# Issuing the gate stores and the rotation's half swaps from ScalarE's queue instead of SyncE's

## The chip, the core and the metric

The kernel runs on one core of one Trainium2 chip. The metric is the device time of one execution in microseconds (us), the median of several runs. The core has a matrix engine (TensorE: PE, with PEld for its weight loads), VectorE (DVE), ScalarE (ACT), GpSimd (POOL) and SyncE (SP). Each engine works through its own list of instructions in order. SP computes nothing; in this kernel it issues nearly all DMAs.

## What is computed

Two encoder layers run over 768 tokens (512 of one request, 256 of another), model width 1024, all in float32. Each layer has three attention branches on the same normalised input:

```python
z = h @ w_in
cq, ckv, kr, gate_a, qkv_b, gate_b, qkv_c, gate_c, merge = jnp.split(z, cuts, axis=-1)
o_a = mla_attention(cq, ckv, kr, g_q, w_uq, g_kv, w_ukv)                       # rotated queries and keys
o_b = dilated_attention(rope(qkv_b[:, :, 0], pos), rope(qkv_b[:, :, 1], pos), qkv_b[:, :, 2])
o_c = neighbourhood_attention(qkv_c[:, :, 0], qkv_c[:, :, 1], qkv_c[:, :, 2], rpb)
mg = jax.nn.sigmoid(merge.reshape(b, s, N_BRANCH, D_MODEL))
mixed = mg[:, :, 0] * p_a + mg[:, :, 1] * p_b + mg[:, :, 2] * p_c               # p_x = (o_x * silu(gate_x)) @ w_px
return x + gate[:, None, :] * rmsnorm(mixed @ w_out, g_post)

def rope(x, pos):       # rotation: each half of a head meets the other half
    x1, x2 = x[..., :half], x[..., half:]
    return jnp.concatenate([x1 * cos - x2 * sin, x2 * cos + x1 * sin], axis=-1)
```

## The kernel before

Features lie on the 128 partitions, tokens along the free axis. A float32 product is made of three matmuls of rounded parts (high by high, high by low, low by high). For that, every weight tile that is loaded (`load_split`, L165) is cast by ACT to its high part (L177), and DVE or POOL subtract to get the low part (L160). `feat_mm` (L201) multiplies such a weight tile with the layer's input; a tile of 1024 weights per partition takes 48 matmuls.

The layers run one after the other, and in each the branches A (`branch_a`), B (`branch_b`) and C (`branch_c`), then `merge` and `project`. The program is written in that order, but a scheduler fixes each engine's list when the kernel is built: it interleaves instructions of neighbouring stages, so where an instruction stands in its engine's list is not where the source has it. Buffers come from pools with fixed numbers of slots.

Two pieces matter here.

**The rotation, `rope_tile` (L448 to L460).** ACT copies a product out of PSUM to `x` (L209, 512 columns and then 256). For the rotation a second tile `xs` is needed, in which the two halves of each head have changed places. Halves lie on different partitions, so `xs` is made by DMAs inside SBUF (L455, L456): four of 32 partitions for a tile of branch B, eight of 16 partitions for a tile of branch A. Then DVE multiplies `x` by the cosines (L458), `xs` by the sines (L459) and adds (L460). Behind that, `q_stack` and `k_stack` split the rotated tile: ACT casts (L409, L421, L422) alternate with DVE subtractions (L410, L423), and PE forms scores (L820). Branch B has 12 such tiles a layer (4 heads by 3 dilations), branch A two; both layers together 24 and 4. In the trace the tiles of branch B are `xb`, those of branch A `qr`.

**The gates ahead, `early` (L1021).** The 24 merge gates of a layer are independent of the attention. Some are computed early, to give PE work while branches wait: `merge_gate` multiplies (tiles `mg`), ACT applies Tanh (L1019) into the tile `the`, which has one buffer, and a DMA stores it to DRAM (L1027). `merge` loads them again. 35 gates go this way.

In the course of branch B, `value_pair` of branch C begins (PE tiles `vp`, L753). Its input is a token permutation of the layer's input, which ACT writes as it casts (`hc`, L923). Exponentials of branch B are L864 on ACT, the casts of its probabilities L879, L884 and L898.

DMAs issued on ACT before: 32 loads of the bias of branch C (L972, L973). All else is issued on SP.

Of the kernel before, what the change touches and what calls it, by code (L numbers as in the profile page):

```python
# [66 lines left out]
def trunk_kernel(ctx, tc, x_t, c_row, c_col, w_ada0, w_ada, cols, w_a, w_feat, w_val, w_val2, w_uqk, w_qr, w_uv, w_pj, w_o,  # L67
                 bias_s, bias_p, rope_t, rope_k, mask_b, mask_c, y_t):
    nc = tc.nc
# [18 lines left out]
    def U(tag, dt=F32, name=None):  # L88
        return pool.tile([P, T], dt, tag=tag, name=name or tag, bufs=BUFS[tag])
# [51 lines left out]
    th_scr = dram.tile([depth, 24, P, T], F32, name="th_scr")  # L141
# [65 lines left out]
    def evac(outs, dst, fn):  # L207
        for g, (o, n) in enumerate(GROUPS):
            fn(dst[:, o:o + n], outs[g])  # L209
# [238 lines left out]
    def rope_tile(outs, cos, sin, half, dst):  # L448

        x = dst  # L450
        xs = U("rp", name="xs")
        if outs:
            evac(outs, x, nc.scalar.copy)
        for b in range(0, P, 2 * half):
            nc.sync.dma_start(out=xs[b:b + half], in_=x[b + half:b + 2 * half])  # L455
            nc.sync.dma_start(out=xs[b + half:b + 2 * half], in_=x[b:b + half])  # L456
        for o, n in GROUPS:
            nc.vector.tensor_mul(x[:, o:o + n], x[:, o:o + n], cos[:, :n])  # L458
            nc.vector.tensor_mul(xs[:, o:o + n], xs[:, o:o + n], sin[:, :n])  # L459
        nc.vector.tensor_add(x, x, xs)  # L460
# [18 lines left out]
    def latents(l, h, hl):  # L479
# [87 lines left out]
        while pend:  # L567
            flip(*pend.pop(0))
        early(l, h, min(LATE_E, FILL[l][0]))
        do_jobs(gates, GATES[l][-1], c_)  # L570
        ada_gain(l)
        pend = [(j, (3, 4, 5)) for j in range(6)]
        early(l, h, FILL[l][0] - LATE_E, lambda k, mm: flips(mm))
        while pend:
            flip(*pend.pop(0))
        return cn, krs

    def branch_a(l, h_, h):
# [13 lines left out]
        va = None  # L592
        for pr in range(4):
            early(l, h, FILL[l][1 + 2 * pr])
            if pr % 2 == 0:

                (wh, wl), = load_split(w_uv[l, pr // 2], 512)[1]
                va = [U("cv", F32R, name="va") for _ in range(4)]
                for t in range(6):
                    vp = ps_mm.tile([P, 256], F32, tag="g1", name="vp")  # L600
                    n = 0
                    for k in range(2):
                        for (a, w) in ((0, wh), (0, wl), (1, wh)):
                            nc.tensor.matmul(vp, cn[3 + k][a][:, t * 128:(t + 1) * 128], w[:, k * 256:(k + 1) * 256],
                                             start=(n == 0), stop=(n == 5))
                            n += 1
                    store_v(va, t, vp)

                outs = feat_mm(w_qr[l, pr // 2], 3, cqn, name="qr")
                qr = U("rp", name="qr")  # L610
                rope_tile(outs, cos_a, sin_a, 16, qr)
                qr_hl = (U("rp", F32R, name="qrh"), U("rp", F32R, name="qrl"))
                nc.scalar.activation(qr_hl[0], qr, AF.Copy, scale=scale)
                nc.vector.scalar_tensor_tensor(qr_hl[1], qr, scale, f(qr_hl[0]), ALU.mult, ALU.subtract)
# [173 lines left out]
    def branch_b(l, h, hl):  # L788
# [4 lines left out]
        for hd in range(4):  # L793
# [10 lines left out]
            for gi, dd in enumerate((1, 4, 16)):  # L804
                outs = feat_mm(w_feat[l, F_B + hd * 3 + gi], KT, hl, name="qkb")
                x = U("rp", name="xb")
                rope_tile(outs, cos_b, sin_b, 32, x)
                xg = lambda g: x[:, GROUPS[g][0]:GROUPS[g][0] + GROUPS[g][1]]
                qs = q_stack(xg, 0, perm_b(dd))
                kb = low(0)  # L810
                ka = k_stack(xg, 1, perm_b(dd), kb, 0)
                prods = ((ka, qs), (kb, qs))
                for g, (o, n) in enumerate(GROUPS):
                    for t2 in range(0, n // P, 2):
                        sp = SP()
                        ts, dst = (pairs[g][t2 // 2] if gi == 0 else ((t2, t2 + 1), None))
                        for k, t in enumerate(ts):
                            q0 = o + (t2 * P if gi else NW[t] if g == 0 else 0)
                            for i, (w, a) in enumerate(prods):
                                nc.tensor.matmul(sp[:, k * 256:k * 256 + 256],  # L820
                                                 w[:, o + t * P:o + t * P + P], a[:, q0:q0 + 256],
                                                 start=(i == 0), stop=(i == 1))
                        if gi == 0 and g == 0:
                            mk = mb0[:, 0:3:2] if t2 == 0 else mb0[:, 1:2].to_broadcast([P, 2, 256])
                            nc.vector.tensor_add(two(dst), two(sp), mk)
                        elif gi == 0:
                            for k in range(2):
                                nc.vector.tensor_add(wins[k], sp[:, k * 256:k * 256 + 256], mb0[:, 2 * k])
                        else:
                            nc.vector.tensor_add(blocks(tbs[g][gi - 1])[:, t2:t2 + 2], blocks(sp)[:, 0:4:3],  # L830
                                                 mbd(gi, g).unsqueeze(1).to_broadcast([P, 2, P]))
# [184 lines left out]
    def merge_gate(l, idx, h, th, between=None):  # L1016
        mg = feat_mm(w_feat[l, F_MG + idx], KT, h, name="mg", between=between)
        for g, (o_, n) in enumerate(GROUPS):
            nc.scalar.activation(th[:, o_:o_ + n], mg[g], AF.Tanh, scale=0.5)  # L1019

    def early(l, h, n, between=None):  # L1021

        for _ in range(n):
            idx = 23 - len(ahead)
            th = U("f", name="the")
            merge_gate(l, idx, h, th, between)
            nc.sync.dma_start(out=th_scr[l, idx], in_=th)  # L1027
            ahead.add(idx)

    def do_jobs(jobs, n, cact):  # L1030
# [167 lines left out]
    xs = []  # L1198
    sums = Z4_()[:, :12].rearrange("p (t c) -> p t c", c=2)
    x2s = [U("cv", name="x2") for _ in range(2)]  # L1200
    for t_ in range(T // P):
        x, x2 = U("cv", name="x"), x2s[t_ // 3][:, t_ % 3 * 256:t_ % 3 * 256 + 256]
        nc.sync.dma_start(out=x, in_=x_t[t_, :, :T])
        if t_ % 3 == 0:
            nc.sync.dma_start(out=x2s[t_ // 3].rearrange("p (t c) -> p t c", c=256),
                              in_=x_t[t_:t_ + 3, :, T:].rearrange("t p c -> p t c"))
# [205 lines left out]
```

## Time and profile before

| | |
|---|---|
| median of 3 runs | 1964.03 us (1962.99 to 1964.36) |
| the profiled execution | 1966.35 us |
| its span, first to last instruction | 1964.6 us |
| PE busy | 1845.0 us, 94% of the span |
| DVE busy | 1530.9 us, 78% |
| ACT busy | 1018.6 us, 52% |
| POOL busy | 664.2 us, 34% |

Busy time is that of the engine's computing instructions. The time in which an engine's queue issues a DMA or waits is not counted as busy, so ACT's 52% leaves out what its queue spends on issuing. The profiled execution is 2.3 us above the median and its time 1.75 us above its span; sums in the prediction are made on the profiled execution and then set against the median.

### The profile page before, as it was taken

What the parts mean: (1) busy time and instruction counts of PE and PEld (TensorE: products, weight loads), DVE (VectorE), ACT (ScalarE), POOL (GpSimd) and SP (SyncE); (2) the same over time, 40 slices, a digit from 0 to 9 for tenths busy, and PEclk for the clock granted to TensorE, in tenths of its full rate; (3) what the DMA queues carried; (4) which work ended last, traced back from release to release, by engine and by line L of the source; (5) the groups of instructions that cost most, each with busy time, mean ns of one, the idle gap of its engine ahead of it and who ended that gap; (6) DMA issues with size and microseconds to landing.
All of it is one profiled execution on the core that took longest, in us unless ns stands there. A gap on an engine that the chain in (4) does not pass through costs nothing. (4 is left out here: it accounts for less than half of the span.)

```text
span 1964.6 us, 30204 instructions
## 1 busy us (share of the span) xinstructions
PE 1845.0 (94%) x10674; PEld 1638.1 (83%) x10674; DVE 1530.9 (78%) x3018; ACT 1018.6 (52%) x2123; POOL 664.2 (34%) x432
## 2 busy tenths in 40 slices
PE   7897999999989987999999999999999999987998
PEld 6886888888877876888999888889888778876898
DVE  8957768579987999896587467687699868997763
ACT  5356556356577455322464356574566684653241
POOL 6404415202221454316534024253022212454570
PEclk9998999999999999999999999999999999998999
DMA  8432241232313233445452332422222222233652
GB/s 294 150 117 62 86 139 57 71 99 82 92 54 92 79 117 115 167 143 191 140 197 89 124 99 88 135 76 86 87 85 85 88 75 89 87 107 99 217 174 71
DMA packets 94904, 221.25 MB, mean 113 GB/s; under 512 B 18096, under 2 KB 32504, under 8 KB 94752
## 3 DMA queue, kind: packets, MB, share of 16 engines
q1 hardware_dynamic: 90144, 213.02, 33.4%
q10 hardware_dynamic: 4608, 6.29, 1.1%
q8 instruction: 84, 1.38, 0.3%
q14 instruction: 68, 0.56, 0.1%
HBM read 173.78 MB, written 28.18 MB: 103 GB/s over the span
## 5 line engine op out<-in xcount | busy, mean ns | idle before, releaser
L665 POOL PARTITION_ALL_REDUCE fixed<-fixed x128 | 314.2, 2486 | 496.3 <-DVE fixed L662 337.0
L201 PE MATMUL mg<-fixed 128*128 128x512 f32 (+1 forms) x2304 | 436.2, 342 | 1.4 <-DVE o_t L397 0.7
L201 PEld LDWEIGHTS mg<-fixed 128*128 128x128 f32 x2304 | 360.3, 191 | 51.6 <-PE sp L984 1.0
L177 ACT CAST fixed<-fixed 128x512 fp32r<-128x512 f32 (+1 forms) x332 | 199.5, 606 | 339.3 <-PE mg L201 117.8
L160 DVE TENSOR_TENSOR fixed<-fixed,fixed 128x512 fp32r<-128x512 f32 (+3 forms) x309 | 224.2, 729 | 113.9 <-ACT fixed L177 110.7
L201 PE MATMUL qkb<-fixed 128*128 128x512 f32 (+1 forms) x1152 | 211.9, 338 | 0.0
L201 PEld LDWEIGHTS qkb<-fixed 128*128 128x128 f32 x1152 | 177.0, 189 | 24.2
L201 PE MATMUL gate<-fixed 128*128 128x512 f32 (+1 forms) x960 | 184.0, 341 | 1.6 <-DVE tq L830 1.3
L201 PEld LDWEIGHTS gate<-fixed 128*128 128x128 f32 x960 | 150.0, 191 | 22.0 <-DVE tq L830 1.5
L1064 PE MATMUL pp<-hi,fixed 128*128 128x512 f32 (+1 forms) x640 | 161.5, 340 | 5.0 <-ACT th L1019 4.7
L680 DVE TENSOR_TENSOR fixed<-tq,fixed 128x512 fp32r<-128x512 f32 (+1 forms) x160 | 127.9, 821 | 2.7 <-ACT fixed L679 2.5
L1064 PEld LDWEIGHTS pp<-hi,fixed 128*128 128x128 f32 x640 | 111.9, 192 | 19.9 <-ACT th L1019 5.1
L671 ACT ACTIVATE tq<-tq 128x512 f32<-128x512 f32 (+1 forms) x160 | 83.4, 545 | 82.7 <-DVE tq L670 82.5
L429 POOL MEMSET kb<- 64x768 f32 x56 | 41.1, 736 | 209.5 <-PE sp L820 121.0
L670 DVE TENSOR_TENSOR tq<-tq,fixed 128x512 f32<-128x512 f32 (+1 forms) x160 | 97.8, 660 | 16.3 <-POOL fixed L665 16.2
L1163 PE MATMUL op<-wo,fixed 128*128 128x384 f32 (+1 forms) x648 | 108.2, 320 | 1.8 <-POOL wo L160 1.8
L1064 PE MATMUL pp<-lo,fixed 128*128 128x512 f32 (+1 forms) x320 | 108.9, 341 | 0.8 <-DVE lo L160 0.8
L1163 PEld LDWEIGHTS op<-wo,fixed 128*128 128x128 f32 x648 | 101.3, 188 | 3.2 <-POOL wo L160 3.1
L311 DVE SCALAR_TENSOR_TENSOR fixed<-tm,fixed 128x768 f32<-128x768 f32 (+1 forms) x128 | 93.3, 729 | 2.1 <-DMA tm<-in_w_ada_dram 0.4
L868 POOL PARTITION_ALL_REDUCE fixed<-fixed x16 | 49.0, 3084 | 128.4 <-DVE fixed L845 65.7
L662 DVE TENSOR_TENSOR fixed<-tq 128x256 f32<-128x256 f32 (+1 forms) x128 | 79.1, 623 | 14.3 <-ACT tq L647 10.8
L679 ACT CAST fixed<-tq 128x512 fp32r<-128x512 f32 (+1 forms) x160 | 80.8, 530 | 11.0 <-PE o_ps L683 8.2
(245 smaller groups left out, 3910.7 us busy)
## 6 DMA issues: line engine op xcount, KB each, us to landing
fixed<-in_w_feat_dram SPq DMA_DIRECT2D x108, 512.0 KB
th_scr<-the SPq DMA_DIRECT2D x35, 384.0 KB
th<-th_scr SPq DMA_DIRECT2D x35, 384.0 KB
tm<-in_w_ada_dram SPq DMA_DIRECT2D x32, 384.0 KB
fixed<-in_w_val_dram SPq DMA_DIRECT2D x20, 512.0 KB
xs<-xb SPq DMA_DIRECT2D x96, 96.0 KB
fixed<-in_w_pj_dram SPq DMA_DIRECT2D x32, 256.0 KB
fixed<-in_w_o_dram SPq DMA_DIRECT2D x16, 512.0 KB
```

The costliest lines, as they stand in the source:

```text
L160: eng.tensor_sub(out, a, b)
L177: nc.scalar.copy(hi[:, :m], raw[:, o:o + m])
L201: state["mm"] = nc.tensor.matmul(outs[g], w[:, wsl], a[g], start=(i == 0 and wi == 0), stop=(i == nk - 1 and wi == 2))
L311: nc.vector.scalar_tensor_tensor(junk, x, 1.0, c, ALU.mult, ALU.mult, accum_out=ada2[:, l, i, g, j:j + 1])
L662: nc.vector.tensor_tensor(out, xs[0], xs[1], op=op)
L665: nc.gpsimd.partition_all_reduce(red, out, P, RED.max if op == ALU.max else RED.add)
L670: nc.vector.tensor_sub(x, x, m)
L671: nc.scalar.activation(x, x, AF.Exp)
L679: nc.scalar.copy(hi, x)
L680: nc.vector.tensor_sub(lo, x, f(hi))
L1064: nc.tensor.matmul(pp, w[:, ws], o[k][a][:, o_:o_ + n], start=(i == 0), stop=(i == 3 * nk - 1))
L1163: mm = nc.tensor.matmul(op[cc], m[a][g][:, k, c0:c0 + P], parts[k][cc][b], start=(k == 0 and i == 0), stop=(k == KT - 1 and i == 2))
```

## The change

Three lines change the queue that issues a DMA. What is moved, from where to where, and how much, stays the same.

```diff
@@ rope_tile
         if outs:
             evac(outs, x, nc.scalar.copy)
         for b in range(0, P, 2 * half):
-            nc.sync.dma_start(out=xs[b:b + half], in_=x[b + half:b + 2 * half])
-            nc.sync.dma_start(out=xs[b + half:b + 2 * half], in_=x[b:b + half])
+            nc.scalar.dma_start(out=xs[b:b + half], in_=x[b + half:b + 2 * half])
+            nc.scalar.dma_start(out=xs[b + half:b + 2 * half], in_=x[b:b + half])
@@ early
             merge_gate(l, idx, h, th, between)
-            nc.sync.dma_start(out=th_scr[l, idx], in_=th)
+            nc.scalar.dma_start(out=th_scr[l, idx], in_=th)
             ahead.add(idx)
```

The scheduler then makes new lists for all engines. Three places on ACT show it. First, the rotation of the first tile of branch A in layer 0 (`xs_1312` from `qr_1311`). In the kernel before, ACT's list has there:

```order
L177 CAST fixed5_72<-fixed15_73 128x512 [waits PE_49,Activation_49]
L209 COPY qr_1311<-qr1_1292 128x256 [waits PE_49]
L409 ACTIVATE qs_1357<-qn1_1338 64x256 [waits PE_49]
L177 CAST fixed5_72<-fixed15_73 128x512 [waits DMAHW0_49,PE_49,Activation_49]
L177 CAST fixed5_72<-fixed15_73 128x512 [waits PE_49,Activation_49]
```

In the changed kernel ACT's list has at the same place:

```order
L209 COPY qr_1311<-qr1_1292 128x256 [waits PE_49]
L455 DMA xs_1312<-qr_1311 16x768 [waits DMAHW6_49,Activation_49]
L409 ACTIVATE qs_1357<-qn1_1338 64x256 [waits PE_49]
L456 DMA xs_1312<-qr_1311 16x768 [waits DMAHW0_49]
L455 DMA xs_1312<-qr_1311 16x768 [waits DMAHW2_49]
L456 DMA xs_1312<-qr_1311 16x768 [waits DMAHW3_49]
L455 DMA xs_1312<-qr_1311 16x768 [waits DMAHW4_49]
L456 DMA xs_1312<-qr_1311 16x768 [waits DMAHW5_49]
L455 DMA xs_1312<-qr_1311 16x768 [waits DMAHW6_49]
L456 DMA xs_1312<-qr_1311 16x768 [waits DMAHW7_49]
L177 CAST fixed5_72<-fixed15_73 128x512 [waits PE_49] x2
```

The eight swaps now stand between the copy and the next weight casts (L177) of ACT.

Second, the eleventh tile of branch B in layer 0 (`xs_5219` from `xb_5218`). In the kernel before, ACT goes from the copy of `xb_5218` to exponentials, and then to the casts of the tile before it (`xb_5117`):

```order
L209 COPY xb_5218<-qkb0_5168 128x512 [waits PE_49]
L209 COPY xb_5218<-qkb1_5169 128x256 [waits PE_49]
L864 ACTIVATE tq_4598<-tq_4598 128x256 [waits DVE_49]
L864 ACTIVATE tq_4599<-tq_4599 128x256 [waits DVE_49]
L864 ACTIVATE tq_4596<-tq_4596 128x256 [waits DVE_49]
L864 ACTIVATE tq_4597<-tq_4597 128x256 [waits DVE_49]
L884 CAST fixed5_72<-tq_4598 128x256 [waits DVE_49,PE_49,Activation_49]
L177 CAST fixed5_72<-fixed15_73 128x512 [waits DMAHW0_49,PE_49]
L409 ACTIVATE qs_5130<-xb_5117 64x512 [waits DVE_49]
```

In the changed kernel ACT has behind the two copies of `xb_5218`:

```order
L455 DMA xs_5219<-xb_5218 32x768 [waits DVE_49,Activation_49]
L409 ACTIVATE qs_5130<-xb_5117 64x512 [waits DVE_49]
L409 ACTIVATE qs_5130<-xb_5117 64x256
L421 CAST ka_5137<-xb_5117 64x512
L422 CAST ka_5137<-xb_5117 64x512
L421 CAST ka_5137<-xb_5117 64x256
L422 CAST ka_5137<-xb_5117 64x256
L456 DMA xs_5219<-xb_5218 32x768 [waits DMAHW1_49]
L864 ACTIVATE tq_4598<-tq_4598 128x256 [waits DVE_49]
L864 ACTIVATE tq_4596<-tq_4596 128x256 [waits DVE_49]
L864 ACTIVATE tq_4599<-tq_4599 128x256 [waits DVE_49]
L455 DMA xs_5219<-xb_5218 32x768 [waits DMAHW2_49]
```

The four swaps of one tile are now spread between computing instructions that wait for DVE; the fourth stands another exponential and a weight cast further down.

Third, the twelfth tile of branch B in layer 0 (`xb_5318`) and the start of branch C's permuting casts (`hc_5549`). In the kernel before, ACT has:

```order
L209 COPY xb_5318<-qkb1_5269 128x256 [waits PE_49]
L898 CAST fixed5_72<-tq_4598 128x2x128 [waits DVE_49,PE_49]
L923 CAST hc_5549<-fixed5_72 128x512
L923 CAST hc_5549<-fixed5_72 128x256
L177 CAST fixed5_72<-fixed15_73 128x512 [waits DMAHW5_49,PE_49]
L409 ACTIVATE qs_5231<-xb_5218 64x512 [waits DMAHW6_49,DVE_49]
```

In the changed kernel ACT has at this place:

```order
L455 DMA xs_5319<-xb_5318 32x768 [waits Activation_49]
L456 DMA xs_5319<-xb_5318 32x768
L455 DMA xs_5319<-xb_5318 32x768 [waits DMAHW6_49]
L456 DMA xs_5319<-xb_5318 32x768 [waits DMAHW7_49]
L177 CAST fixed5_72<-fixed15_73 128x512 [waits PE_49]
L409 ACTIVATE qs_5231<-xb_5218 64x512 [waits DVE_49]
L409 ACTIVATE qs_5231<-xb_5218 64x256
L421 CAST ka_5238<-xb_5218 64x512 [waits Pool_49]
L422 CAST ka_5238<-xb_5218 64x512
L421 CAST ka_5238<-xb_5218 64x256
L422 CAST ka_5238<-xb_5218 64x256
L923 CAST hc_5549<-fixed5_72 128x512 [waits DMAHW3_49,DMAHW2_49,DMAHW1_49]
```

The four swaps and the six casts of `xb_5218` now stand ahead of the first cast of `hc`.

## Rows read from the trace of the kernel before

**Rows 1.** The page's busy times: us, share of the span, instructions.
```profile
PE 1845.0 (94%) x10674; PEld 1638.1 (83%) x10674; DVE 1530.9 (78%) x3018; ACT 1018.6 (52%) x2123; POOL 664.2 (34%) x432
```

**Rows 2.** What PE waited for: us in total, times, longest.
```profile
PE sp L820 <- DVE kb L423: 5.9, 5, 2.1
PE vp L753 <- ACT hc L923: 5.7, 4, 2.8
...
PE sp L820 <- ACT ka L422: 4.8, 7, 1.3
```

**Rows 3.** Stretches of layer 0: length, busy PE, PEld, DVE, ACT, POOL; clock; DMA share, GB/s.
```profile
387.00:450.00 63.00, 63.00 (x380) 55.85 (x379) 47.36 (x85) 36.00 (x68) 4.33 (x4) 1.00 0.30 90
450.00:540.00 90.00, 85.11 (x518) 74.82 (x517) 84.51 (x144) 51.76 (x90) 22.56 (x14) 1.00 0.28 87
540.00:570.00 30.00, 25.68 (x139) 21.39 (x138) 29.48 (x53) 21.67 (x40) 8.25 (x3) 0.89 0.27 73
570.00:615.00 45.00, 39.33 (x188) 31.70 (x188) 33.56 (x63) 39.40 (x64) 10.03 (x6) 1.00 0.19 60
```

**Rows 4.** Issues by tile and line: duration in ns (min/median/max), first and last start.
```profile
L455 SPq DMA_DIRECT2D xs<-xb x48: 507/542/593, 394.5 to 1562.0; - x48
L456 SPq DMA_DIRECT2D xs<-xb x48: 581/590/1672, 395.1 to 1562.7; - x48
L456 SPq DMA_DIRECT2D xs<-qr x16: 578/589/900, 130.5 to 1262.4; - x16
L1027 SPq DMA_DIRECT2D th_scr<-the x35: 319/327/530, 111.0 to 1728.3; - x35
L972 ACTq DMA_DIRECT2D bm<-in_bias_s_dram x16: 334/334/384, 599.5 to 1682.2; - x16
```

**Rows 5.** Waits of ACT and DVE for DMAs: us in total, times, longest.
```profile
ACT fixed L177 <- DMA fixed<-in_w_feat_dram: 2.0, 2, 1.4
DVE xb L458 <- DMA xs<-xb: 6.9, 4, 1.9
```

**Rows 6.** ACT in order of time where the second and third place lie.
```profile
541.51 0.84 ACT L209 COPY xb<-qkb 128x512 f32<-128x512 f32 x2
542.25 1.34 ACT L864 ACTIVATE tq<-tq 128x256 f32<-128x256 f32 x4
...
546.66 0.94 ACT L409 ACTIVATE qs<-xb 64x512 fp32r<-64x512 f32 x2 [1.75 <-DVE xb L460]
...
549.33 0.41 ACT L422 CAST ka<-xb 64x256 fp32r<-64x256 f32 x1
...
551.66 1.70 ACT L923 CAST hc<-fixed 128x512 fp32r<-128x512 f32 x2
```

**Rows 7.** SP's queue, the swaps of the eleventh tile.
```profile
542.37 0.51 SPq L455 DMA_DIRECT2D xs<-xb  x1
...
544.20 0.59 SPq L456 DMA_DIRECT2D xs<-xb  x1
```

**Rows 8.** DVE, the eleventh tile: first product and sum of the rotation.
```profile
549.00 0.70 DVE L458 TENSOR_TENSOR xb<-xb,fixed 128x512 f32<-128x512 f32 x1
...
555.18 0.95 DVE L460 TENSOR_TENSOR xb<-xb,xs 128x768 f32<-128x768 f32 x1
```

**Rows 9.** PE where branch C's value products begin.
```profile
561.96 0.49 PE L753 MATMUL vp<-fixed,hc 128*128 128x512 f32 x1 [2.76 <-ACT hc L923]
```

**Rows 10.** ACT and its queue around a bias load that it issues.
```profile
599.40 0.63 ACT L923 CAST hc<-fixed 128x256 fp32r<-128x256 f32 x1
599.52 0.38 ACTq L972 DMA_DIRECT2D bm<-in_bias_s_dram  x1
599.94 0.41 ACT L864 ACTIVATE tq<-tq 128x256 f32<-128x256 f32 x1
```

**Rows 11.** ACT, the casts behind the first rotation of branch A.
```profile
131.76 1.14 ACT L177 CAST fixed<-fixed 128x512 fp32r<-128x512 f32 x2 [1.51 <-PE kn L201]
```

**Rows 12.** PE, the gate whose weights those casts make.
```profile
138.82 8.51 PE L201 MATMUL mg<-fixed 128*128 128x512 f32 x48
```

## Prediction

> **What bounds the kernel now.** I read the page's busy times first. PE computes for 94% of the span, DVE for 78%, ACT for 52% [rows 1]: the kernel is bound by PE, and time is gained or lost where PE stands still. So the second view is the list of PE's waits. None of its large entries ends on a DMA; the ones that touch the changed code are waits for the casts and subtractions behind the rotation, 5.9 + 4.8 us, and for the permuted input of branch C, 5.7 us [rows 2].
>
> The third view is busy time by stretch, for layer 0's branch B, where 12 of a layer's 14 rotated tiles are. The reader is to see three situations [rows 3]. From 387 to 450 us PE is busy for all 63 us: whatever others do there is hidden. From 450 to 540 us PE has 4.9 us idle of 90, DVE is busy for 84.5, ACT for 51.8. From 540 to 615 us branch B runs into branch C: PE is idle for 4.3 of 30 and then 5.7 of 45 us, and ACT is busy for 39.4 of those 45. There ACT is what is waited for; the last 2 of the layer's 12 tiles fall there. In the stretch from 540 to 570 us the granted clock is 0.89 of full speed: part of it runs at the lower of the two levels (1.2 instead of 2.4 GHz), after PE had stood idle. That costs 30 x 0.11 = 3.3 us.
>
> **What the change moves, and its cost.** The issues go from SP to ACT. On SP a swap of branch B takes 0.542 and 0.590 us in turn, so four take 2.26 us; eight swaps of branch A, at 0.589, take 4.7 us; a store of a gate takes 0.327 us [rows 4]. The trace of before has no swap on ACT. It has bias loads there, 0.334 us each [rows 4], the same as what SP needs for a transfer over 128 partitions, so I take SP's durations for ACT. In total ACT's queue gets 24 x 2.26 = 54.3 us, 4 x 4.7 = 18.8 us and 35 x 0.327 = 11.4 us, together 84.5 us, which raises what it has to do from 1018.6 to 1103 us, 56% of the span. That is far from a bound as a sum, so the place decides.
>
> An issue on ACT can cost nothing: a bias load was issued from 599.52 to 599.90 us while ACT computed from 599.40 to 600.03, and the next instruction followed at 599.94 [rows 10]. But a swap reads what ACT has just copied and waits for that copy (the wait on Activation in the new lists), so ACT has run dry when the first swap goes out, and four swaps in a row leave it with nothing for up to 2.26 us. Bounds for each tile: 0 and 2.26 us.
>
> What SP wins: nothing that is waited for. ACT waited 2.0 us in all for the weight loads of `w_feat` that share SP with the moved issues [rows 5]. Bounds 0 and -2.0; I take 0.
>
> *Stores (11.4 us)* are single issues behind a Tanh, like the bias loads: 0, with 11.4 as the far end.
>
> *Branch A's swaps (18.8 us).* The first place in the lists shows 8 swaps ahead of the weight casts that stood at 131.76 us [rows 11]. The copy ended at about 129.6, so they would start at 129.6 + 4.9 = 134.5, 2.8 us later, be done by 135.7, and the low halves on DVE by about 137. PE needs these weights at 138.82 [rows 12]. Hidden, with some 2 us to spare: 0. If that cover is gone, up to 4.7 us for each of four tiles.
>
> *Branch B, first five tiles of each layer* (22.6 us): PE is full [rows 3], 0.
>
> *Branch B, middle five tiles of each layer* (10 x 2.26 = 22.6 us). ACT has room (38 us of 90), but casts on ACT and subtractions on DVE alternate, DVE is nearly full, and in the new lists the four swaps of a tile are mostly not in a row: in 22 of 24 tiles an instruction that waits for PE or DVE stands between them. Then the tile's last swap is late by that wait. Between 0 and 22.6 us I take a quarter, 5.6, since PE has other matmuls in its list for most of such a delay.
>
> *Branch B, last two tiles of layer 0.* The swaps of the eleventh tile were issued from 542.37 to 544.79 us [rows 7], and DVE took up the tile at 549.00 [rows 8]. In the new list the second swap stands behind the casts of the tile before, whose last one ended at 549.74 [rows 6], and the fourth behind four exponentials and a weight cast besides. From 549.74 that is 0.59 + 1.34 + 0.54 + 0.62 + 0.59 = 3.7 us, so the last swap would be out at 553.4 us. A swap needs time to land; DVE waited at most 1.9 us for one [rows 5]. So DVE could begin at about 555, 6 us late, with its sum (now 555.18, rows 8) late by less, because DVE was busy with other work between the two. Bounds 0 and 6; I take half, 3. For the twelfth tile the four swaps, 2.26 us, go ahead of the first `hc` cast, which started at 551.66 [rows 6] and for which PE waited 2.76 us at 561.96 [rows 9]: taken whole, 2.3. Layer 1's list is like it in kind but differs in order; I take half of its 2 x 2.26, 2.3. Together 7.6.
>
> Sum: 5.6 + 7.6 = 13.2 us. On the profiled execution that is 1966.4 + 13.2 = 1979.6 us. The median of the runs shown lies 2.3 us below that execution, so I forecast **1977 us**.
>
> **The rivals.**
>
> *Nothing to be measured* (chance 0.20). ACT is idle for 48% of the span, PE has filler work, and all 84.5 us vanish: 1964 us. The stretches with a full PE speak for it, the last stretch with ACT at 39.4 of 45 us against it. A run of this kernel tells a difference from none at about 0.2%, 3.9 us, so this is 1960 to 1968. The Trainium skill has a rule for it (DMA: Bandwidth & Descriptors, "Issuing engines are not separate DMA queues"): whichever engine starts a DMA, the same 16 engines carry it, and another issuer saves only sequencer time. By that rule alone nothing is gained, since SP's time is not what is waited for; the trace agrees with the premise in the 2.0 us above, and the rule doesn't price what the issues cost on a computing engine.
>
> *Faster* (0.16). Swaps no longer stand in SP's list behind loads, and go out from the queue of the engine that made their data. If the rotation's tiles come earlier where PE waits for their casts, the 5.9 + 4.8 us of such waits [rows 2] go: 1964 - 10.7 = 1953 us. It decides if a swap now is late at its source. Against it: at the eleventh tile SP issued the first swap at 542.37 us, 0.02 after the copy's end (541.51 + 0.84, rows 6 and 7), and DVE waited 6.9 us in total for swaps of branch B [rows 5]. The Trainium skill states (same page, "Queues, rings and completion order") that each DMA engine takes turns between the queue rows it has work for. By that a swap on ACT's row would pass loads queued on SP's; no run here shows it yet, and its worth is bounded by the 6.9 us.
>
> *Much slower* (0.14). The swaps that stand behind waiting instructions on ACT make DVE late, DVE makes ACT's next casts late, and PE's filler runs out. Then all issue time of branch B outside the full stretch lands, 14 x 2.26 = 31.6 us, and two more stalls put the clock at its lower level at 3.3 us each: 1964 + 38 = 2002 us. The 22 of 24 tiles speak for it; that ACT has 38 us of 90 free in the middle stretch speaks against.
>
> **How the numbers follow.** My forecast's case has 0.50 and spans 1969 to 1990: from the 5 us that the end of layer 0 gives alone to twice the sum. All of it and the heavy case are slower by over 0.2%: 0.64. Within 0.2%: 0.20. Faster: 0.16. The range of 8 in 10 reaches from 1956, which leaves out the better half of the fast case, to 1998, which leaves out the heavy case from near its middle.
>
> **What the profile after would show.** Issue rows of the swaps on ACT's queue at about 0.54 and 0.59 us, of the stores at 0.33. ACT's busy time unchanged near 1019 us, since issuing isn't counted, but with gaps of 1 to 2.3 us behind the copies of L209. From 387 to about 450 us PE still full. From 540 to 615 us more PE idle time than 10 us, before `vp` and the scores L820, by some 5 us, and DVE's waits for swaps above 6.9 us. If instead DVE's waits for swaps shrink and the scores wait less, the fast rival holds. The forecast is wrong if the new lists, which differ on every engine and far from the rotation too, move a stall elsewhere that I haven't priced, or if ACT issues a swap in much more or less than 0.6 us.

## The result and the profile after

The changed kernel takes **1984.7 us** (median of 4 runs, 1979.6 to 1987.1) against 1964.2 for the kernel before (median of 4): a ratio of **1.0101** (95% interval 1.0081 to 1.0122), 20.5 us slower. The forecast was 1977 us, slower, within 1956 to 1998. The profiled execution is the fastest of the four (1979.55 us); its span is 1977.8 us, 13.2 us above that of before, so the profile shows less than the medians' 20.5 us. One execution among those of e10 below, of 9460 us, counts as slow and is left out of its ratio.

Of the page's busy times, which answer to [rows 1], only PE's moves by more than 2 us. For the same 10674 products it is up by 8.1 us, and the mean granted clock is 0.974 where it was 0.978; the other 5.1 of the 13.2 us are idle time of PE:

```profile
PE 1853.1 (94%) x10674; PEld 1642.4 (83%) x10674; DVE 1528.9 (77%) x3018; ACT 1017.4 (51%) x2123; POOL 663.9 (34%) x432
```

The issues by line (columns as in [rows 4]) show the swaps and stores on ACT's queue at the prices taken from SP:

```profile
L455 ACTq DMA_DIRECT2D xs<-xb x48: 514/515/1556, 393.4 to 1566.8; - x48
L456 ACTq DMA_DIRECT2D xs<-xb x48: 514/602/1901, 393.9 to 1572.2; - x48
L456 ACTq DMA_DIRECT2D xs<-qr x16: 514/600/872, 131.0 to 1271.3; - x16
L1027 ACTq DMA_DIRECT2D th_scr<-the x35: 326/327/358, 111.6 to 1735.0; - x35
```

The waits (us in total, times, longest) say where work is late now. DVE waits twice as long for swaps of branch B as in [rows 5]; ACT waits before weight casts where the eight swaps of branch A go out (a wait that wasn't there); of PE's old waits [rows 2] those for the casts behind the rotation fell (4.8 to 2.2 us for `ka`), and others took their place: `o_ps` behind `o_t` (3.5 us before), `o_ps` behind L898 (2.8 before) and `qn` (none before):

```profile
DVE xb L458 <- DMA xs<-xb: 14.0, 7, 3.4
ACT fixed L177 <- DMA xs<-qr: 14.1, 3, 5.2
PE o_ps L683 <- DVE o_t L397: 11.3, 4, 4.9
PE o_ps L902 <- ACT fixed L898: 8.2, 8, 2.9
PE qn L201 <- DVE va L709: 4.3, 1, 4.3
PE sp L820 <- ACT ka L422: 2.2, 4, 0.9
```

The stretches of [rows 3], after:

```profile
387.00:450.00 63.00, 63.00 (x380) 55.51 (x378) 46.32 (x80) 34.83 (x63) 7.15 (x5) 1.00 0.30 88
540.00:570.00 30.00, 25.36 (x137) 21.74 (x136) 28.76 (x49) 21.31 (x38) 8.03 (x6) 0.89 0.25 71
570.00:615.00 45.00, 37.87 (x174) 31.15 (x174) 33.49 (x54) 39.69 (x61) 11.84 (x6) 0.89 0.14 47
```

Fixed windows mislead once work has shifted. So I measure a stretch between PE's own marks, the first and the last start of a tile's products, from rows like these:

```profile
L201 PE MATMUL qkb<-fixed x576: 274/337/404, 381.9 to 548.0; 128*128 128x512 f32 x96, 128*128 128x256 f32 x96
L753 PE MATMUL vp<-fixed,hc x144: 387/389/794, 564.2 to 619.4; 128*128 128x512 f32 x144
L201 PE MATMUL qr<-hi,fixed x24: 279/336/404, 1114.4 to 1260.7; 128*128 128x512 f32 x12, 128*128 128x256 f32 x12
L201 PE MATMUL qkb<-fixed x576: 274/337/404, 1389.3 to 1564.0; 128*128 128x512 f32 x96, 128*128 128x256 f32 x96
```

Four stretches come out: branch B of layer 0 (first to last `qkb`, 166.1 us here), its passage into branch C (last `qkb` to last `vp` on `hc`, 71.4), branch A of layer 1 (first `qr` to first `qkb`, 274.9) and branch B of layer 1 (174.7). For before they are 164.3, 65.3, 267.1 and 178.3. So +1.8, +6.1, +7.8 and -3.6: together 12.1 of the 13.2 us. Each number comes from one execution of each kernel, and the executions of the changed kernel alone lie up to 7.5 us apart, so a difference of two or three us in one stretch says little. The loss sits in the passage, as forecast, and in branch A of layer 1, which was priced at nothing. There PE stands still at two places:

```profile
1265.25 0.53 PE L201 MATMUL qn<-hi,fixed 128*128 128x256 f32 x1 [4.32 <-DVE va L709]
1323.50 0.77 PE L683 MATMUL o_ps<-fixed,va 128*128 128x512 f32 x1 [3.88 <-DVE o_t L397]
```

Neither names ACT or a swap. DVE's own list around the first (start, duration, idle time before):

```profile
1255.65 0.23 DVE L690 RECIPROCAL fixed<-fixed 128x12 f32<-128x12 f32 x1 [4.30 <-DMA fixed<-den_scr]
1261.58 0.96 DVE L655 TENSOR_TENSOR o_t<-o_t,den 128x768 f32<-128x768 f32 x1 [3.53 <-DMA den<-rden_scr]
1263.45 0.61 DVE L709 TENSOR_TENSOR va<-vp,va 128x256 fp32r<-128x256 f32 x2
```

DVE waits for a round trip through DRAM (the softmax denominators of the pair before), and the subtractions that free PE's banks stand behind it. Before, DVE waited there about as long (2.56 + 5.10 us against 4.30 + 3.53), and PE only 0.47 us:

```profile
1246.74 0.23 DVE L690 RECIPROCAL fixed<-fixed 128x12 f32<-128x12 f32 x1 [2.56 <-DMA fixed<-den_scr]
1253.18 0.96 DVE L655 TENSOR_TENSOR o_t<-o_t,den 128x768 f32<-128x768 f32 x1 [5.10 <-DMA den<-rden_scr]
```

```profile
1255.60 0.39 PE L201 MATMUL qr<-hi,fixed 128*128 128x256 f32 x1 [0.47 <-DVE va L709]
```

PE's list then began the `vp` products at 1245.17 us, 1.6 before that reciprocal; now at 1249.54, 6.1 before it: the work that covered the wait is used up earlier. That points to the order rather than the queue.

### The profile page after: what moved, and what is told of

Read it like the earlier page. It is cut to its first block, busy times and chain, and to the rows that moved or that the text cites. A ratio compares the mean times of both kernels' runs of the same rounds, so it can differ in the third digit from the quotient of the medians.

```text
span 1977.8 us, 30120 instructions
## 1 busy us (share of the span) xinstructions
PE 1853.1 (94%) x10674; PEld 1642.4 (83%) x10674; DVE 1528.9 (77%) x3018; ACT 1017.4 (51%) x2123; POOL 663.9 (34%) x432
## 5 line engine op out<-in xcount | busy, mean ns | idle before, releaser
L201 PE MATMUL mg<-fixed 128*128 128x256 f32 (+1 forms) x2304 | 438.8, 341 | 1.8 <-DVE o_t L397 0.7
L177 ACT CAST fixed<-fixed 128x512 fp32r<-128x512 f32 (+1 forms) x332 | 198.2, 606 | 293.9 <-PE mg L201 89.6
L680 DVE TENSOR_TENSOR fixed<-tq,fixed 128x512 fp32r<-128x512 f32 (+1 forms) x160 | 121.7, 781 | 2.4 <-ACT fixed L679 2.2
```

Of the source, the lines that this page charges most:

```text
L177: nc.scalar.copy(hi[:, :m], raw[:, o:o + m])
L201: state["mm"] = nc.tensor.matmul(outs[g], w[:, wsl], a[g], start=(i == 0 and wi == 0), stop=(i == nk - 1 and wi == 2))
L680: nc.vector.tensor_sub(lo, x, f(hi))
```

## The experiments

Ratios are to the kernel before on the same chip, with 95% intervals. Two questions: which part costs, and is it ACT's issue time, with what it delays (theory 1), or the new order of the lists (theory 2)?

**Parts alone.**

```diff
+            q = nc.scalar if half == 16 else nc.sync      # e3; half == 32 in e4
-            nc.sync.dma_start(out=xs[b:b + half], ...)
+            q.dma_start(out=xs[b:b + half], ...)
```

e1 moves both kinds of swaps, e2 only the stores.

> All 112 swaps on ACT's queue, the 35 stores left on SP's. Theory 1 (ACT's in-order list: swaps hold the casts behind them and come late themselves behind casts that wait; the swaps carry the whole loss): as the full change, 1.007 to 1.013 of the kernel before, about 1984 us, with the same two places of loss, some 9 us in layer 1's branch A and some 6 us where branch B of layer 0 runs into branch C. Theory 2 (a new interleaving of all lists, whatever is moved, costs by chance): anything from 0.995 to 1.015, and not the same two places. Theory 3 (the stores cost as much as the swaps): about 1.005.

> Only the 35 stores on ACT's queue, the swaps left on SP's. Theory 1: 11.4 us of issue time behind Tanhs cost nothing that shows, 0.998 to 1.002. Theory 2: up to 1 per cent either way although only single issues move, since all lists are made anew. Theory 3: 1.005 or more.

> Only the 32 swaps of branch A (four tiles of eight) on ACT's queue. The prediction's step priced them at nothing: 0.998 to 1.002. If the place that the changed kernel's trace shows (the second tile of layer 1, about 9 us lost by the time branch B begins) is the work of these eight swaps: 1.003 to 1.006, with the loss at that place, and ACT waiting there for swaps before its weight casts. If the loss there came of the new order that the swaps of branch B or the stores brought: no loss there now.

> Only the 96 swaps of branch B on ACT's queue. The prediction's steps give them the whole loss, 13 us: 1.006 to 1.008. If branch A's swaps carry the loss of layer 1: about 6 us at the end of layer 0's branch B and little else, 1.002 to 1.004. Theory 2 (new interleaving alone): the two halves, this run and the one with branch A's swaps, don't add up to the run with all swaps.

Measured: all swaps 1.0070 (1.0054 to 1.0086); stores 1.0012 (1.0000 to 1.0023); branch A's swaps **1.0055** (1.0042 to 1.0069); branch B's swaps **0.9991** (0.9981 to 1.0002). That is the forecast upside down: moved alone, each part under lists of its own, the 18.8 us of issues priced at nothing cost 11 us, and the 54.3 us priced at 13.2 cost nothing. The parts multiply to 1.0058, not 1.0101. And the stall before `qn` (4.3 us) is there with the stores alone, while one near 1320 us comes with branch A's swaps (3.29 us before `o_ps` in e1; 4.18 us in e3, there before `sp`). Theory 2 gains.

**Is it the time that branch A's swaps take?** e5 swaps the blocks in reverse order, e6 leaves half of the swaps on SP, e7 keeps all on SP but cuts each in two by columns. e8 is the change without branch A's swaps.

```diff
+        for b in range(0, P, 2 * half)[::-1 if half == 16 else 1]:      # e5
-            nc.sync.dma_start(out=xs[b:b + half], ...)                  # e6: only the first of each pair
+            q.dma_start(out=xs[b:b + half], ...)
+        for c in ((0, 384), (384, 768)) if half == 16 else ((0, 768),):  # e7
```

> Only branch A's swaps on ACT's queue, as in e3_swaps_a, but the four blocks of a tile are swapped in the reverse order. The issue time on ACT is the same, the lists come out anew. Theory 1 (ACT stands for some 5 us per tile between the copy and its next weight casts): the loss stays, 1.004 to 1.007. Theory 2 (the loss of e3_swaps_a is a chance of that interleaving): anywhere from 0.997 to 1.007, with the stalls at other places.

> Branch A's swaps shared: four of a tile on ACT's queue, four on SP's. ACT stands for some 2.4 us per tile instead of 5, and the last swap goes out some 2.5 us earlier. Theory 1: half the loss of e3_swaps_a or less, 1.000 to 1.003, and ACT's next weight cast some 2.5 us earlier than there. Theory 2: no order in the issue time, anything from 0.997 to 1.007.

> All swaps on SP's queue, but branch A's each cut in two of 384 columns, so 16 issues per tile: ACT is free of them, and the last one goes out some 4.5 us later than before. If what costs is that ACT is held: 0.998 to 1.002. If the loss in e3_swaps_a comes from the rotated tile being late on DVE: at least as much as there, 1.005 or more, since the tile is later here (by about 4 us; there by 1 to 4).

> The change without branch A's swaps: stores and branch B's swaps on ACT's queue, branch A's on SP's. If the parts add up (stores 1.0012, branch B 0.9991): 0.999 to 1.002, and branch A's swaps are what makes the change slow. If parts meet each other (the whole change measured 1.010, its parts 1.0012, 0.9991 and 1.0055): 1.003 to 1.006.

Measured: e5 1.0039 (1.0025 to 1.0054); e6 1.0019 (1.0009 to 1.0029); e7 0.9997 (0.9987 to 1.0007); e8 **1.0052** (1.0038 to 1.0065). Fewer issues on ACT, less loss: e3 and e6 fit theory 1. e5 cannot tell the theories apart: in its trace every engine computes in the very order of e3, so it is e3's loss a second time. In e3 the weight casts that followed the copy of `qr` after 0.4 us in the kernel before (first two rows) now follow after 5:

```profile
1257.57 0.39 ACT L209 COPY qr<-qr 128x256 f32<-128x256 f32 x1
1258.34 1.14 ACT L177 CAST fixed<-fixed 128x512 fp32r<-128x512 f32 x2
```

```profile
1260.68 0.39 ACT L209 COPY qr<-qr 128x256 f32<-128x256 f32 x1
1266.14 1.86 ACT L177 CAST fixed<-fixed 128x512 fp32r<-128x512 f32 x4 [4.10 <-PE gate L201]
```

PE does not wait for those casts. It waits 1.0 us for the rotated tile, at 1279.13 us, and longer only after that, for DVE:

```profile
1317.11 0.80 PE L645 MATMUL sp<-qs,ka 128*128 128x512 f32 x1 [4.18 <-DVE u L440]
```

That the held casts lead to this stall is not shown. e7 doesn't tell what it was made for: the first eight issues of a tile went out ahead of the copy of its second group of columns, and the last one ended 5.0 us after that copy, as before, so the tile was not late. e8 speaks for theory 2: two parts that cost 1.0012 and 0.9991 alone cost 1.0052 together. Both theories hold somewhere; they had to be taken apart.

**Queue and lists apart.** The scheduler is given the order: each engine's list is read from one build and tied, instruction to instruction, into another. These ties only fix the order on an engine; they add no wait. The traces show that they held: in e9, e10 and e12 PE, DVE, ACT and POOL compute in exactly the order of the build they were tied to. In e11 DVE's list was left to the scheduler, and 64 of its 3018 instructions stand elsewhere than before. A kernel tied to its own lists was not run.

```diff
         trunk_kernel(tc, *args)
+        _pin(nc, tc)      # for each engine, over its list of the other build:
...
+            tc.add_manual_dep(i, prev.name, NoSync)
```

> The full change (all swaps and stores on ACT's queue), but PE, DVE, POOL, ACT's computing instructions and SP's remaining DMAs are held to the order of the lists of the kernel before; only the 147 moved issues are new on ACT. Theory 1 (the issue time on ACT itself holds casts back): as the full change, 1.007 to 1.013. Theory 2 (the new lists that the scheduler makes cost the time, above all the two stalls of layer 1's branch A, where PE stood 4.3 us before the product qn and 3.9 us before the second product o_ps): 0.998 to 1.004, without the first of these stalls. Both in part: 1.004 to 1.007.

> The reverse: all swaps and stores on SP's queue as before, but the computing instructions of every engine and SP's other DMAs are held to the order of the lists of the changed kernel. Theory 1: 0.997 to 1.002, since ACT issues none of it. Theory 2: as the full change, 1.006 to 1.012, with both stalls of layer 1's branch A. Both in part: 1.002 to 1.006.

> Only branch B's 96 swaps on ACT's queue, with PE, POOL, ACT's computing instructions and SP's remaining DMAs held to the lists of the kernel before (DVE's list is left to the scheduler). With lists of its own this part measured 0.9991. If branch B's swaps do hold ACT back and new lists hid that: 1.004 to 1.008, with the wait of PE for branch B's casts near 426 us that e9_new_queue_old_lists shows (2.3 us), and again in layer 1. If branch B's swaps cost nothing under any lists: 0.998 to 1.002.

> All swaps and stores on SP's queue as before, all lists held to those that the scheduler made for e4_swaps_b (which measured 0.9991 with 54 us of issue time on ACT). If those lists are better than the old ones by about what branch B's issues cost: 0.993 to 0.997, faster than both kernels. If they are worth nothing and the issues cost nothing under them: 0.998 to 1.001.

| queue | lists | moved to ACT | ratio | 95% interval |
|---|---|---|---|---|
| ACT | own | all (the change) | 1.0101 | 1.0081 to 1.0122 |
| ACT | of before | all (e9) | 1.0106 | 1.0086 to 1.0125 |
| SP | of the change | nothing (e10) | 1.0053 | 1.0035 to 1.0070 |
| ACT | own | branch B's swaps (e4) | 0.9991 | 0.9981 to 1.0002 |
| ACT | of before, but for DVE's | branch B's swaps (e11) | 1.0056 | 1.0041 to 1.0072 |
| SP | of e4 | nothing (e12) | **0.9952** | 0.9937 to 0.9968 |

Both effects are real. With everything on SP, the new lists alone lose 0.53%, with the same two stalls:

```profile
1260.99 0.55 PE L201 MATMUL qn<-hi,fixed 128*128 128x256 f32 x1 [4.28 <-DVE va L709]
1318.80 0.76 PE L683 MATMUL o_ps<-fixed,va 128*128 128x512 f32 x1 [3.89 <-DVE o_t L397]
```

With the old lists, ACT's issues lose 1.06%; beside the lists of the change they cost 1.0101 / 1.0053 = 1.0048. So the two don't add up: on SP the change's lists cost 0.53%, but once ACT issues, old and new lists come out alike (1.0106, 1.0101). Branch B's swaps cost 1.0056 under the old lists, and 0.9991 / 0.9952 = 1.0039, 8 us (by the two intervals some 4 to 11), under lists that happen to be better by 0.48%. Those lists hid the cost in e4. e12 beats both kernels: 1958.1 us in the median, against 1966.6 for the kernel before on its chip, with no DMA moved.

The stretches measured between PE's marks, in us against before:

| | B, layer 0 | passage | A, layer 1 | B, layer 1 |
|---|---|---|---|---|
| the change | +1.8 | +6.1 | +7.8 | -3.6 |
| e10: SP, lists of the change | +0.3 | +6.0 | +7.0 | -5.6 |
| e12: SP, lists of e4 | -1.7 | +6.2 | -2.2 | -7.0 |
| e9: ACT, old lists | +5.9 | +0.2 | -0.2 | +7.1 |
| e11: ACT, old lists, branch B | +5.4 | +1.1 | -2.9 | +6.1 |

Read by rows it is plain: what the change loses in the passage and in layer 1's branch A comes with the lists, whichever queue issues. What ACT's issues cost under the old lists lands in branch B: 13.0 of e9's 18.8 us. Another 4.0 lie between branch C of layer 0 and branch A of layer 1, and were not traced. DVE's waits for branch B's swaps, 14.0 us in the change, are no measure of the queue by themselves: with everything on SP the change's lists have 12.7 (e10). With the lists held they rise from 6.9 [rows 5] to 17.4 us (before, e9) and from 10.6 to 15.4 (e12, e4).

How it lands there is to be seen in e9 at the third tile of layer 0, in the stretch where PE was full. ACT and its queue, then SP's queue:

```profile
415.26 0.85 ACT L209 COPY xb<-qkb 128x512 f32<-128x512 f32 x2
...
416.15 0.51 ACTq L455 DMA_DIRECT2D xs<-xb  x1
...
418.00 0.61 ACTq L456 DMA_DIRECT2D xs<-xb  x1
```

```profile
416.11 0.33 SPq L165 DMA_DIRECT2D fixed<-in_w_feat_dram  x1
```

The swaps go out as promptly as before, 0.04 us behind the copy (before: 0.02). But SP has no swaps to issue any more, and starts its next weight load, 512 KB, 0.04 us ahead of the first swap. The DMA queues from 416.7 to 418.8 us (packets, MB, share of the 16 engines) show only SP's queue (q1) at work, though three more swaps were issued in that time; ACT's queue (q10) moves only after it:

```profile
q1 hardware_dynamic: 97, 0.40, 80.1%
...
xs<-xb ACTq DMA_DIRECT2D x3, 96.0 KB
```

```profile
q10 hardware_dynamic: 192, 0.39, 63.6%
```

In the kernel before SP issued that load behind the four swaps, at 417.31 us. DVE, in e9 and before:

```profile
421.78 0.69 DVE L458 TENSOR_TENSOR xb<-xb,fixed 128x512 f32<-128x512 f32 x1 [3.43 <-DMA xs<-xb]
```

```profile
418.93 0.69 DVE L458 TENSOR_TENSOR xb<-xb,fixed 128x512 f32<-128x512 f32 x1 [1.44 <-DMA xs<-xb]
```

From the end of the last issue to DVE's product it is 421.78 - 418.61 = 3.2 us, and was 418.93 - 417.21 = 1.7. The rest of DVE's delay against before, 1.35 us, is as large as the first tile's already was (1.39 us). There the load went out 0.45 us behind the first swap, and from 396.3 to 397.5 us its packets ran alone:

```profile
394.29 0.54 ACTq L455 DMA_DIRECT2D xs<-xb  x1
...
396.15 0.61 ACTq L456 DMA_DIRECT2D xs<-xb  x1
```

```profile
394.74 0.33 SPq L165 DMA_DIRECT2D fixed<-in_w_feat_dram  x1
```

```profile
399.94 0.69 DVE L458 TENSOR_TENSOR xb<-xb,fixed 128x512 f32<-128x512 f32 x1 [3.03 <-DMA xs<-xb]
```

That is 399.94 - 396.76 = 3.2 us again; before, it was 398.55 - 396.98 = 1.6. ACT's queue is not slow in itself. In the changed kernel one tile's swaps had the DMA engines to themselves from 1521.7 us on, and DVE, which stood waiting, took the tile up 1.8 us after the last issue:

```profile
1521.32 0.60 ACTq L456 DMA_DIRECT2D xs<-xb  x1
```

```profile
1523.72 0.69 DVE L458 TENSOR_TENSOR xb<-xb,fixed 128x512 f32<-128x512 f32 x1 [2.00 <-DMA xs<-xb]
```

Back in e9, the casts follow late, and PE waits where it had not; the window behind that wait has a granted clock of 0.83, part of it at the lower level, where the kernel before had 1.00 (second row below; the columns of [rows 3]):

```profile
428.53 0.51 PE L820 MATMUL sp<-qs,ka 128*128 128x256 f32 x2 [2.33 <-ACT ka L422]
```

```profile
430.00:440.00 10.00, 10.00 (x51) 8.69 (x51) 8.36 (x17) 3.25 (x9) 3.59 (x3) 0.83 0.34 93
```

```profile
430.00:440.00 10.00, 10.00 (x59) 8.70 (x58) 9.04 (x19) 4.95 (x13) 3.60 (x3) 1.00 0.30 92
```

## Why the prediction was right in its range and wrong in its steps

- **Prices of the issues** (0.54, 0.59, 0.33 us; 84.5 us in all): right (the change's 147 issues take 88.0 us), and ACT's busy time stayed at 1017 us.
- **Branch A's swaps, 0**: the step that failed first. Moved alone they cost 1.0055; the two microseconds "to spare" held at the first tile (PE goes into `mg` at 139.52 us without a gap) and said nothing of the second tile of a layer. How much of it is their issue time and how much the lists is open for this part: branch A's swaps under the old lists alone were not run. In e9, where they stand on ACT under the old lists with all the rest, layer 1's branch A is as long as before (-0.2 us) and has neither stall, which speaks for the lists.
- **Branch B, middle five tiles, 5.6, and first five, 0**: all of branch B's swaps, priced at 13.2, cost some 8 to 11 us (e12 to e4, and e11), so a cost is there and not far off in size, but its place and its way were wrong: PE was full in the first five only because its work arrived in time, and under the old lists PE waits there, 2.33 us in layer 0. In e9 DVE takes up layer 0's fifth tile 4.0 us later than before (451.01, 446.99), the ninth 4.1 (519.15, 515.02) and the twelfth 5.6 (562.70, 557.06). So in that layer most of the delay arises where 0 was forecast, and in the two tiles traced above it comes of swaps that land late, not of swaps issued late. A full engine is no proof of slack behind it.
- **Branch B, last two tiles, 7.6**: right place, wrong cause. The passage is 6.1 us longer, but also 6.0 and 6.2 with everything on SP (e10, e12), and 0.2 to 1.1 with ACT's issues under the old lists. What I read out of the new list as the swaps' delay was the list's.
- **Stores, 0**: 1.0012 alone, at the edge of what can be told. Together with branch B's swaps they cost far more (e8 beside e4); which of the lists' turns that was is not settled.
- **What SP wins, 0**: the sign was missed. SP's free queue lets loads start earlier, in front of the swaps or among them. The faster rival had it that swaps on a queue of their own pass SP's loads; e9 shows one behind a load. The Trainium skill (DMA: Bandwidth & Descriptors, "Queues, rings and completion order") says that an engine finishes a whole packet of one row's descriptors before it turns to the next row. What the trace shows fits that: between 416.7 and 418.8 us 97 packets of q1, none of q10. I had used only the turn-taking.
- **The term that was missing**: the lists themselves. The prediction named it under what could make it wrong ("a stall elsewhere that I haven't priced") and gave it no number. With everything on SP they cost 0.53%, half of the 1.01%. The 13.2 us of the forecast met 13.2 us of span by luck: the lists' stalls, priced at nothing, stand where delays of the swaps were priced that did not come there, and the profiled execution is the fastest of four. By the medians the loss is 20.5 us.

Not settled: why the scheduler's order for the change is worse than that of before, and that for e4 better. Three orders of one program, on the same queues, span 1.0053 to 0.9952.

## What to carry to other kernels

Where a scheduler orders the program, moving a DMA to another queue is two changes: hold the lists fixed and move the queue, then hold the queue and move the lists, before either is believed. Moving DMAs off a queue also moves up what stood behind them there; look at which transfer will then be in front. And a change whose parts are measured as harmless (0.9991) can be a cost of 0.4% that a lucky order pays for; the order is then worth keeping without the change.

## What was not expected of the hardware

Eight swaps of 16 partitions on ACT's queue go out 0.64 us apart and hold ACT's weight casts for their whole length (5.0 us at 1261.1 to 1266.1 us in e3). A swap that shares the DMA engines with a 512 KB load started 0.04 us earlier was used 3.2 us after its issue instead of 1.7, and so was one whose load started 0.45 us behind the first of its four swaps (3.2 instead of 1.6).
